# Two of four convolution tiles' input projections, and a third modulation vector, move from ahead of the attention blocks to the gaps between their heads

## The chip, the cores and the metric

The kernel runs on one core of one Trainium2 chip. Its engines are named as the profile names them: PE (TensorE, matmuls; PEld is its weight load), DVE (VectorE), ACT (ScalarE), POOL (GpSimd) and SP (SyncE, which here issues nearly all transfers). The metric is the device time of one execution in microseconds (us). Before the change three runs took 1443.88, 1449.33 and 1449.51 us, median 1449.33 us.

## What is computed

One inference step of a two-layer backbone on 640 tokens (512 latent, 128 context), width 1024, all in float32. The change touches the first (even) layer's mixer, cut here to its core:

```python
mp = _adaln(cond_ctx, w_mod[li], b_mod[li])     # six modulation vectors per layer and token group
hs = _modulate(y_s, norm_mix[li], ms[0], ms[1])
q, k, v, u = _even_split(hs, w_in)              # one input projection: 512 + 128 + 128 + 1024 columns
o_att  = _latent_attention(rope(q), rope(k), v, ck, cv, sink)   # windows of 384 or 512 keys, sink logit
o_conv = silu(_layernorm(_dwconv(a * sigmoid(gate), w, b)))     # a, gate = split(u); width 31, 512 channels
y_s = y_s + ms[2] * (concat([o_att, o_conv]) @ w_out)
y_s = y_s + ms[5] * (relu(_modulate(y_s, norm_ffn, ms[3], ms[4]) @ w1) ** 2) @ w2
```

The second (odd) layer has an RG-LRU in place of attention and convolution; both layers end with the squared-ReLU MLP. The context tokens go through the same steps, with their own modulation.

## The kernel before

Channels lie on the 128 partitions and tokens along the free dimension: `x` is 128 x 8 x 640. Float32 products are made of three matmuls on split operands (high x high, high x low, low x high), so a projection of 128 output channels, a **unit**, is 48 matmuls of 320 to 322 columns (`product`, L113, called by `att_unit`). `weights` loads the unit's 512 KB (`wraw`), ACT makes the high part (`whi`, L98), DVE the low one (`wlo`, L66).

The even layer runs in this order. The first modulation group and the norm. Then units for the four convolution tiles (two units each, value and gate), for keys, values and four query pairs: `conv_in(0)`, `conv_in(1)`, `key`, `value`, `query(0..3)`, `conv_in(2)`, `conv_in(3)`. `conv_in` multiplies the value by the sigmoid of the gate. Tiles 0 and 1 are convolved on DVE (`conv_gen`, 31 steps L409 each), tiles 2 and 3 on PE (`PE_CONV`): 16 small ACT copies (L466) bring the tile into the form `up`, and `conv_mm` runs 36 matmuls (L423; two records each in the trace) for it, 16 ACT copies (L428) take the result out.

Then five attention blocks of 128 queries: the context block first (128 keys), then latent blocks with 384, 512, 512 and 384 keys. A block goes through four head groups: `scores` (PE, six matmuls into a two-bank PSUM tile of `P2()`), `reduced` (DVE, L563: mask and running maximum, writes the scores to a slot of `S_all`), and after the fourth `softmax` (ACT: exponentials L573, scaling L579). `emit_values` of the block before it transposes the weights on PE (L599), copies them (ACT, L600, `th`) and multiplies with the values (L603); its result goes to `qh` and `ql` (ACT L606, DVE L66).

`filler(n)` takes n steps from the list `fill` between these pieces. A modulation step (`mod_gen`) is one 512 KB load `mraw` from `wmod` with two buffers, and four short matmuls (L292; eight records); 16 steps make one group of two modulation vectors. Before the change `fill` holds group (0,1), the two `conv_mm`, and group (0,2). Groups (1,0), (1,1), (1,2) of the next layer are filled into the MLP of layer 0, one step per unit. The layer norm of the convolution (`layer_norm`: ones-matmuls L627 and L645) runs in the last blocks. After attention, `out_proj` runs 16 products of 24 matmuls, 8 on the attention's result, 8 on the convolution's, and DVE adds them to `x` (L142).

`S_all` takes the two 16 KB buffers `hl` and `hh` that held the normed input, 16 slots of 512. PSUM has two tiles `p2`, one `p3` (every third `P2()` while `third()` is open) and two `p1`.

The program is written in one order, and a list scheduler settles each engine's order from it, moving instructions up where their operands are ready. On the chip each engine takes its own list in order, and waits where an operand or a buffer isn't ready.

## Time and profile before

| | us |
|---|---|
| median of three runs | 1449.33 |
| the profiled execution | 1448.39 |
| its span, first to last instruction | 1446.6 |
| mean granted TensorE clock | 0.985 of 2.4 GHz |
| the four units of `conv_in(2)` and `conv_in(3)` | 104.4 to 132.7 |
| the attention blocks | 132.7 to 256.2 |
| the output projection | 256.2 to 319.5 |
| the MLP of layer 0, its first quarter | 319.5 to 437 |

PE is busy for 1395.1 us of the span, DVE 1012.8, ACT 762.0. A stretch view gives the busy time of each engine in it, the granted clock (1.00 is 2.4 GHz, half of it 1.2 GHz), the busy share of the 16 DMA engines and what they moved. PE's busy time counts a matmul from its start to its modelled end; PEld shows how much of a stretch weights were loaded in. The chain of waits follows the last instruction back through what released each one.

### The profile page before, as it was taken

Reading aid. Unit: us, or ns where it says so; the run is one execution under the profiler, and the core shown is the slowest. Engines: PE = TensorE matmul, PEld = TensorE weight load, DVE = VectorE, ACT = ScalarE, POOL = GpSimd, SP = SyncE. Lnnn points to the kernel's source line nnn. Section 1 sums busy time; section 2 is a strip of 40 time slices with the busy share of each in tenths; the row PEclk is TensorE's granted clock in tenths of the full one; section 3 lists DMA queues with packets and bytes.
Section 4 is the critical chain, followed back from the end, with each engine's and each line's share of the span. In section 5 each row is a group of like instructions: output and inputs, shape, how many; then the busy total and the mean of one; then the engine's idle time right before and its main releaser. Section 6 shows DMA issues by size and latency. Waiting matters only on the chain.

```text
span 1446.6 us, 23553 instructions
## 1 busy us (share of the span) xinstructions
PE 1395.1 (96%) x9525; PEld 1301.3 (90%) x9525; DVE 1012.8 (70%) x1846; ACT 762.0 (53%) x1232; POOL 37.9 (3%) x57
## 2 busy tenths in 40 slices
PE   7999898999999999999999999899999999999998
PEld 4998563999989999999989999899999999999997
DVE  6699533675775675675687689997686676676673
ACT  5335788455534533543555878835643543543553
POOL 0000000000000000000000023210000000000000
PEclk9999799999999999999999999999999999999998
DMA  8623634124254334334213122122213113113112
GB/s 327 230 76 126 210 136 161 59 88 131 88 173 148 102 132 175 117 117 175 73 59 102 59 73 74 58 74 88 73 45 121 70 58 116 60 59 117 44 59 73
DMA packets 44061, 156.60 MB, mean 108 GB/s; under 512 B 5040, under 2 KB 5808, under 8 KB 43952
## 3 DMA queue, kind: packets, MB, share of 16 engines
q1 hardware_dynamic: 43952, 155.09, 30.9%
q8 instruction: 75, 1.23, 0.3%
q14 instruction: 34, 0.28, 0.1%
HBM read 152.31 MB, written 2.76 MB: 107 GB/s over the span
## 4 chain that ended last, share of the span: by engine, by line
PE 82%; DVE 7%; ACT 7%; DMA 2%; issue 1%; SPq 0%; ACTq 0%
PE p L113 65%; PE bu L113 11%; PE p L292 3%; DMA mraw<-in_wmod 2%; DVE wlo L66 1%; PE p L423 1%; DVE ib L1022 1%; DVE xc L963 1%; ACT whi L98 1%; ACT S L573 1%; PE p L603 1%; ACT z L428 1%; DVE ib L1015 1%; ACT hh L186 1%; DVE t L1014 0%
## 5 line engine op out<-in xcount | busy, mean ns | idle before, releaser
L98 ACT ACTIVATE whi<-wraw 128x512 fp32r<-128x512 f32 (+1 forms) x327 | 246.4, 779 | 440.7 <-PE p L113 323.2
L113 PE MATMUL p<-hh,whi 128*128 128x320 f32 (+1 forms) x1512 | 462.4, 313 | 2.8 <-ACT hh L186 1.7
L113 PE MATMUL p<-hl,whi 128*128 128x320 f32 (+1 forms) x1512 | 460.1, 311 | 0.2 <-DVE hl L187 0.2
L113 PE MATMUL p<-hh,wlo 128*128 128x320 f32 (+1 forms) x1512 | 350.5, 311 | 0.0
L66 DVE TENSOR_TENSOR wlo<-wraw,whi 128x512 fp32r<-128x512 f32 (+1 forms) x327 | 279.9, 879 | 48.4 <-ACT whi L98 46.9
L113 PEld LDWEIGHTS p<-hh,whi 128*128 128x128 f32 x1512 | 286.1, 189 | 15.4 <-issue 7.8
L113 PEld LDWEIGHTS p<-hl,whi 128*128 128x128 f32 x1512 | 286.4, 189 | 0.9 <-DVE hl L187 0.8
L113 PEld LDWEIGHTS p<-hh,wlo 128*128 128x128 f32 x1512 | 256.8, 189 | 0.9 <-issue 0.8
L113 PE MATMUL p<-fh,whi 128*128 128x320 f32 x528 | 166.4, 315 | 4.0 <-ACT whi L98 1.1
L113 PE MATMUL p<-fl,whi 128*128 128x320 f32 x528 | 163.3, 309 | 2.0 <-DVE fl L66 2.0
L113 PE MATMUL p<-fh,wlo 128*128 128x320 f32 x528 | 163.1, 310 | 0.7 <-DVE wlo L66 0.7
L142 DVE SCALAR_TENSOR_TENSOR x<-p,mod,x 128x320 f32<-128x320 f32 (+2 forms) x228 | 96.3, 451 | 54.6 <-PE p L113 51.7
L268 DVE TENSOR_TENSOR fr<-p,R 128x640 f32<-128x640 f32 x64 | 52.7, 823 | 101.6 <-PE p L113 101.6
L113 PE MATMUL bu<-fh,whi 128*128 128x320 f32 x360 | 112.5, 313 | 0.3 <-ACT bu L828 0.3
L113 PEld LDWEIGHTS p<-fh,whi 128*128 128x128 f32 x528 | 99.2, 188 | 14.0 <-issue 5.1
L113 PE MATMUL bu<-fl,whi 128*128 128x320 f32 x360 | 111.5, 310 | 0.0
L113 PE MATMUL bu<-fh,wlo 128*128 128x320 f32 x360 | 111.5, 310 | 0.0
L727 ACT ACTIVATE fr<-fr,bs 128x512 f32<-128x512 f32 (+1 forms) x128 | 65.2, 554 | 78.6 <-DVE bs L270 78.4
L113 PEld LDWEIGHTS p<-fl,whi 128*128 128x128 f32 x528 | 99.3, 188 | 2.4 <-DVE fl L66 2.4
L113 PEld LDWEIGHTS p<-fh,wlo 128*128 128x128 f32 x528 | 99.1, 188 | 1.5 <-DVE wlo L66 1.5
L292 PE MATMUL p<-mraw,base 128*32 128x256 f32 x768 | 66.6, 425 | 16.0 <-DMA mraw<-in_wmod 9.0
L113 PEld LDWEIGHTS bu<-fh,whi 128*128 128x128 f32 x360 | 68.0, 189 | 2.2 <-issue 1.2
(220 smaller groups left out, 1999.0 us busy)
## 6 DMA issues: line engine op xcount, KB each, us to landing
wraw<-in_w_ff SPq DMA_DIRECT2D x128, 512.0 KB, 3.5
mraw<-in_wmod SPq DMA_DIRECT2D x96, 512.0 KB, 4.2
wraw<-in_w_li SPq DMA_DIRECT2D x16, 512.0 KB, 3.4
wraw<-in_w_att SPq DMA_DIRECT2D x14, 512.0 KB, 3.6
cw<-in_w_cv SPq DMA_DIRECT2D x8, 576.0 KB, 4.3
wraw<-in_w_ao SPq DMA_DIRECT2D x8, 512.0 KB, 3.5
wraw<-in_w_lo SPq DMA_DIRECT2D x8, 512.0 KB, 3.5
x<-in_xT SPq DMA_DIRECT2D x4, 640.0 KB, 9.1
```

What stands on the lines that cost most here:

```text
L66: nc.vector.tensor_tensor(out, full, f32(hi), op=ALU.subtract)
L98: nc.scalar.activation(hi, raw, AF.Copy)
L113: nc.tensor.matmul(o, w, v, start=start, stop=stop, **kw)
L142: nc.vector.scalar_tensor_tensor(v, src[:, a:b], gate[:, n, s:s + 1], v, op0=ALU.mult, op1=ALU.add)
L186: nc.scalar.activation(h, v, AF.Copy, scale=S[:, kt, s:s + 1])
L268: nc.vector.tensor_tensor(hy(o), p[:, :, 0:320], R, op=ALU.mult)
L292: nc.tensor.matmul(p[32 * q:32 * q + 32, half * 256:half * 256 + 256], base[:, kt], raw[:, q * 256:q * 256 + 256], start=(kt == 0), stop=( ...
L423: nc.tensor.matmul(o, w[:, b], U[j][:, g, b:b + 164], start=b == 0, stop=b == 8)
L428: nc.scalar.activation(zv[32 * g:32 * g + 32, s], o[32 * s:32 * s + 32], AF.Copy)
L573: nc.scalar.activation(S[g][:, :N], S[g][:, :N], AF.Exp, bias=mx[:, g:g + 1], scale=1.0, accum_out=ss[:, g:g + 1])
L603: nc.tensor.matmul(pav[c], vv[:, sl, c], th[:, b.kv], start=(j == 0), stop=(j == len(vs) - 1))
L727: nc.scalar.activation(r[:, a:b], r[:, a:b], AF.Relu, bias=bs[:, q:q + 1])
```

## The change

- `conv_in(2)` and `conv_in(3)` leave the place ahead of attention. They become `conv_in_steps`: a step is one eighth of a unit (six matmuls), in the one tile `p3`. With the two `conv_mm` they form a second list, `work`.
- A `gap(m, w)` takes three steps of DVE's convolution, m modulation steps and w steps of `work`. It stands after every head group (before: after every second one), after every slice of `emit_values`, and after every block.
- Group (1,0) of the next layer's modulation joins `fill` ahead of attention; the MLP of layer 0 keeps (1,1) and (1,2).
- The normed input must now live through the blocks, so `S_all` is six slots of a new tile `S_own` (two of them first hold the rope table) and ten slots in `x` itself. After the last block `x` is loaded again, four 640 KB transfers on POOL's queue.
- In the blocks `p3` belongs to `work`, so scores and transposes share the two `p2`. `th` and its kin have two buffers instead of three. The convolution's weights come in 12 pieces of 192 KB a tile (four buffers), not four of 576 KB (two buffers).
- The layer norm of the convolution moves into the first half of the output projection.
- `Norm.finish` writes its two sums into one `p2` tile, where it had two `p1`, when it runs in another stage than the norm's (three times).

```diff
-    def product(p, wh, wl, cols, rhs):
+    def product(p, wh, wl, cols, rhs, first=True, last=True):
...
+            w = None if one else P2()
             for h in range(2):
-                p = P1()
-                nc.tensor.matmul(p[:, 0:320], ones, self.acc[:, h * 320:h * 320 + 320], start=True, stop=True)
-                nc.vector.tensor_scalar(v[:, h], p[:, 0:320], 1.0 / 1024, 1e-6, op0=ALU.mult, op1=ALU.add)
+                p = P1()[:, 0:320] if one else w[:, h, 0:320]
+                nc.tensor.matmul(p, ones, self.acc[:, h * 320:h * 320 + 320], start=True, stop=True)
...
+            if not one:
+                nc.vector.tensor_scalar(v, w[:, :, 0:320], 1.0 / 1024, 1e-6, op0=ALU.mult, op1=ALU.add)
...
+    S_own = bp.tile([128, 6, 512], F32, name="S")
+    rope = S_own[:, 4:6]
+    xs = x.rearrange("p k t -> p (k t)")
+    S_all = [S_own[:, i] for i in range(6)] + [xs[:, i * 512:i * 512 + 512] for i in range(10)]
...
+    def conv_in_steps(j):
+        t = []
+        for i in (2 * j, 2 * j + 1):
+            wh, wl = weights(w_att[i])
+            p = spare[0].tile([128, 2, 512], F32, name="p3", tag="p3")
+            for k in range(8):
+                product(p, wh, wl, [k], [rhs[k]], k == 0, k == 7)
+                yield
+            a = ap_.tile([128, 640], F32, name="tg", tag="t", bufs=4)
+            t += [a, normed(a, p)]
+        conv_u(j, None, None, t)
+        yield
...
-    conv_in(2)
-    conv_in(3)
-    fill.append(mod_gen(0, 1, mp))
+    use_spare.pop()
+    work.extend(conv_in_steps(j) for j in PE_CONV)
+    work.extend(conv_mm(j) for j in PE_CONV)
+    fill.extend([mod_gen(0, 1, mp), mod_gen(0, 2, mp), mod_gen(1, 0, mp)])
...
+    GAPS = [((1, 2), None, (1, 2))] + [((1, 2), (1, 1), (1, 1))] * 4
+    def gap(m, w):
+        conv_step(3)
+        filler(m)
+        filler(w, work)
+    gap(4, 4)
     for i, pair in enumerate(blocks):
         for g in range(4):
             scores(pair, g)
-            if g % 2:
-                filler(F2)
+            gap(*GAPS[i][0])
         if i:
-            emit_values(i - 1)
+            emit_values(i - 1, GAPS[i][1])
         for b in pair:
             b.softmax()
...
+        gap(*GAPS[i][2])
     conv_step(200)
-    emit_values(4)
-    filler(100)
-    for _ in ln:
-        pass
+    filler(100, work)
+    emit_values(4, (1, 0))
+    for k in range(0, 8, 2):
+        nc.gpsimd.dma_start(x[:, k:k + 2], xT[:, k:k + 2])
+    use_spare.append(1)
...
     for t in range(4):
+        next(ln, None)
         out_proj(w_ao, t, qr, lambda n, p: add_gated(n, p, G))
+        if t == 1:
+            for _ in ln:
+                pass
...
-        for g in range(3):
+        for g in range(1, 3):
             fill.append(mod_gen(1, g, mp))
```

What stands where, at three places. On PE, before, at the end of the last of the four units and the start of the context block; p3_1188 is the unit's tile, p1_1274 the modulation's, p2_1311 and p2_1326 the first two score tiles:

```order
L113 MATMUL p3_1188<-hl_157,whi_1184 128x322
L113 MATMUL p3_1188<-hh_156,wlo_1185 128x320
L113 MATMUL p3_1188<-hh_156,wlo_1185 128x322
L292 MATMUL p1_1274<-mraw_1275,base_77 32x256 x4
L292 MATMUL p1_1274<-mraw_1281,base_77 32x256 x4
L113 MATMUL p2_1311<-kh_230,qh_228 128x128 x2
L113 MATMUL p2_1311<-kl_231,qh_228 128x128 x2
L113 MATMUL p2_1311<-kh_230,ql_229 128x128 x2
L113 MATMUL p2_1326<-kh_230,qh_228 128x128 x2
```

And now, where the first score tile (p2_1043) stands inside the first of those units (p3_1018), with modulation steps (pm_987) between:

```order
L305 MATMUL pm_987<-mraw_1000,base_77 32x256 x4
L119 MATMUL p3_1018<-hh_156,whi_1014 128x322
L119 MATMUL p3_1018<-hl_157,whi_1014 128x322
L119 MATMUL p3_1018<-hh_156,wlo_1015 128x320
L119 MATMUL p3_1018<-hh_156,wlo_1015 128x322
L119 MATMUL p2_1043<-kh_230,qh_228 128x128 x2
L119 MATMUL p2_1043<-kl_231,qh_228 128x128
L305 MATMUL pm_987<-mraw_1006,base_77 32x256 x4
L119 MATMUL p2_1043<-kl_231,qh_228 128x128
L119 MATMUL p2_1043<-kh_230,ql_229 128x128 x2
L119 MATMUL p3_1018<-hh_156,whi_1014 128x320
```

The blocks begin four units earlier in PE's list, and the four units are spread to the third block; 44 modulation steps stand between them and the last transposes, where there were 32.

On ACT, before, around the first exponentials (L573): both sigmoids (L450, `sgm`) and both runs of copies `up` are done ahead of the one table load:

```order
L450 ACTIVATE sgm<-sgm,bs 128x512
L450 ACTIVATE sgm<-sgm,bs 128x128
L466 ACTIVATE up<-u 32x172 x16
L573 ACT_TABLE_LOAD
L573 ACTIVATE S,ss<-S,mx 128x128 x4
L575 ACTIVATE es<-es 128x4
L573 ACTIVATE S,ss<-S,mx 128x128 x3
L579 ACTIVATE S<-S,ss 128x128 x4
```

And now, after the context block's scaling (L618), ahead of the first latent block's exponentials (L612); `tg` is the gate:

```order
L618 ACTIVATE x<-x,ss 128x128
L104 ACTIVATE whi<-wraw 128x1024
L490 ACT_TABLE_LOAD
L490 ACTIVATE tg<-tg,bs 128x512
L490 ACTIVATE tg<-tg,bs 128x128
L506 ACTIVATE up<-u 32x172 x16
L639 ACTIVATE th<-p_1389 128x1024
L612 ACT_TABLE_LOAD
L612 ACTIVATE x,ss<-x,mx 128x384
L646 ACTIVATE qh<-p_1387 128x4x128
```

The same comes once more in the third block, so the blocks hold five table loads where they held one, and both runs of 16 copies.

On PE at the start of the MLP of layer 0, before, the norm's two sums (L209) between the first two units (p2_2864, p2_2948):

```order
L113 MATMUL p2_2864<-hh_2541,wlo_2861 128x322
L113 MATMUL bu0_2856<-hh_2541,whi_2860 128x320
L113 MATMUL bu1_2857<-hh_2541,whi_2860 128x320
L209 MATMUL p1_2918<-sq_2583,ones_70 128x320
L209 MATMUL p1_2921<-sq_2583,ones_70 128x320
L113 MATMUL p2_2948<-hh_2541,whi_2944 128x320
```

And now, the sums in a p2 tile (p2_3031); the next unit's tile (p2_3057) has the same PSUM address:

```order
L119 MATMUL bu1_2970<-hh_2654,whi_2973 128x320
L219 MATMUL p2_3031<-sq_2696,ones_70 128x320 x2
L305 MATMUL pm_2042<-mraw_3280,base_77 32x256 x4
L119 MATMUL p2_3057<-hh_2654,whi_3053 128x320
```

The second unit stands behind DVE's reading of the sums, with one modulation step between.

## Rows read from the trace of the kernel before

**Rows 1.** The head of the page: the span, busy time of PE, ACT and DVE with share and instruction count, and the clock that the throttle granted in 40 slices (tenths).

```profile
span 1446.6 us, 23553 instructions
PE 1395.1 (96%) x9525; PEld 1301.3 (90%) x9525; DVE 1012.8 (70%) x1846; ACT 762.0 (53%) x1232; POOL 37.9 (3%) x57
...
PEclk9999799999999999999999999999999999999998
```

**Rows 2.** Stretches of the four units, the blocks, the output projection and the MLP's first quarter, then the blocks in three parts: length, busy us of PE, PEld, DVE, ACT and POOL (instructions), granted clock, DMA share, GB/s.

```profile
104.40:132.70 28.30, 28.30 (x193) 28.11 (x191) 27.09 (x40) 15.11 (x26) 0.00 (x0) 1.00 0.22 75
132.70:256.20 123.50, 105.56 (x710) 62.21 (x710) 60.08 (x175) 93.97 (x209) 0.00 (x0) 0.89 0.49 170
256.20:319.50 63.30, 63.30 (x434) 63.30 (x433) 48.48 (x95) 34.34 (x50) 0.00 (x0) 1.00 0.22 75
319.50:437.00 117.50, 117.50 (x836) 108.11 (x836) 78.25 (x139) 52.73 (x85) 0.00 (x0) 1.00 0.40 134
132.70:180.00 47.30, 39.57 (x264) 24.70 (x264) 32.37 (x85) 34.40 (x87) 0.00 (x0) 0.78 0.62 216
180.00:220.00 40.00, 36.42 (x251) 23.76 (x253) 12.98 (x43) 32.55 (x68) 0.00 (x0) 0.96 0.34 123
220.00:256.20 36.20, 29.56 (x205) 13.75 (x198) 14.73 (x47) 27.03 (x57) 0.00 (x0) 0.95 0.48 160
```

**Rows 3.** Who waited for whom in the blocks (132.7 to 256): us in total, times, the longest.

```profile
ACT S L573 <- DVE mx L570: 9.1, 4, 6.2
...
ACT z L428 <- PE p L423: 7.0, 5, 3.0
...
PE p L292 <- DMA mraw<-in_wmod: 5.6, 6, 1.4
...
PE p L423 <- ACT z L428: 4.1, 5, 1.4
...
PE p L292 <- DVE mx L563: 1.9, 1, 1.9
...
PE p L113 <- DVE bs L270: 1.6, 1, 1.6
```

**Rows 4.** Pieces of the chain of waits on PE, start us and length: six units in a row; then, in the blocks, a modulation step and a group of 18 convolution records at either clock, six score matmuls, 12 records of values, eight transposes.

```profile
90.14 42.63 PE p L113 x288
...
144.30 1.01 PE p L292 x8
...
175.87 4.45 PE p L423 x18
...
180.89 2.71 PE p L423 x18
183.59 0.92 PE p L113 x6
...
216.84 2.89 PE p L603 x12
...
239.49 1.02 PE p L599 x8
...
243.37 0.57 PE p L292 x8
```

**Rows 5.** Groups on ACT in the blocks, by line and shape: busy us, mean ns of one.

```profile
L466 ACT ACTIVATE up<-u 32x172 f32<-32x172 f32 x17 | 8.7, 513 | 1.4 <-DVE u L456 1.3
...
L634 ACT ACTIVATE zsq<-z 128x656 f32<-128x656 f32 x4 | 2.8, 735 | 0.0
...
L573 ACT ACT_TABLE_LOAD x1 | 1.3, 1283 | 0.0
L98 ACT ACTIVATE whi<-wraw 128x1024 fp32r<-128x1024 f32 x1 | 1.1, 1059 | 0.0
L450 ACT ACTIVATE sgm<-sgm,bs 128x512 f32<-128x512 f32 x1 | 0.7, 722 | 1.9 <-DVE bs L270 1.9
L450 ACT ACTIVATE sgm<-sgm,bs 128x128 f32<-128x128 f32 x1 | 0.4, 387 | 0.0
```

**Rows 6.** ACT in order of time around that table load: start us, us.

```profile
145.76 1.02 ACT L466 ACTIVATE up<-u 32x172 f32<-32x172 f32 x2
146.80 1.28 ACT L573 ACT_TABLE_LOAD   x1
148.10 0.40 ACT L573 ACTIVATE S<-S,mx 128x128 f32<-128x128 f32 x1
```

**Rows 7.** Pieces of the chain in which the `mraw` load itself was waited for: start us, us from issue to landing.

```profile
133.83 5.64 DMA mraw<-in_wmod
...
220.36 3.53 DMA mraw<-in_wmod
...
232.70 4.25 DMA mraw<-in_wmod
```

**Rows 8.** The chain from the end of the blocks into the MLP of layer 0: the layer norm's sums (L627, L645), the output projection, the norm's sums (L209), units and modulation steps.

```profile
240.51 0.86 PE p L627 x2
...
241.94 0.42 PE p L627 x2
...
252.88 1.06 PE p L645 x2
...
255.80 0.42 PE p L645 x2
256.22 63.42 PE p L113 x432
...
319.93 1.08 PE p L209 x4
...
329.44 7.32 PE p L113 x48
336.76 0.57 PE p L292 x8
337.33 7.32 PE p L113 x48
```

**Rows 9.** DVE at that norm, in order of time: start us, us, idle before.

```profile
320.51 1.03 DVE L210 TENSOR_SCALAR nv<-p 128x320 f32<-128x320 f32 x2 [1.74 <-PE p L209]
```

**Rows 10.** Issues of transfers on the page: count, KB each, median us to landing.

```profile
mraw<-in_wmod SPq DMA_DIRECT2D x96, 512.0 KB, 4.2
...
x<-in_xT SPq DMA_DIRECT2D x4, 640.0 KB, 9.1
```

More of the change, by code (lines that the diff above doesn't have):

```diff
@@ L43, in backbone @@
     ps = ctx.enter_context(tc.tile_pool(name="ps", bufs=1, space=PSUM, reuse_waits="tile"))
-    spare, turn_ = [], count()
+    spare, use_spare, turn_ = [], [], count()
     @contextmanager
@@ L50, in third @@
             spare.append(pool)
+            use_spare.append(1)
             yield
             spare.pop()
+            use_spare.clear()
     def P2():
-        if spare and next(turn_) % 3 == 2:
+        if use_spare and next(turn_) % 3 == 2:
             return spare[0].tile([128, 2, 512], F32, name="p3", tag="p3")
         return ps.tile([128, 2, 512], F32, name="p2", tag="p2", bufs=2)
+    ones_, both_ = count(), []
     def P1():
-        return ps.tile([128, 512], F32, name="p1", tag="p1", bufs=2)
+        t = "p1b" if both_ and next(ones_) % 2 else "p1"
+        return ps.tile([128, 512], F32, name="p1", tag=t)
     def f32(ap):
@@ L113, in mm @@
         nc.tensor.matmul(o, w, v, start=start, stop=stop, **kw)
-    def product(p, wh, wl, cols, rhs):
+    def product(p, wh, wl, cols, rhs, first=True, last=True):
         n = len(cols)
         for i, (c, ((ha, hb), (la, lb))) in enumerate(zip(cols, rhs)):
-            s, e = i == 0, i == n - 1
+            s, e = first and i == 0, last and i == n - 1
             cs = slice(c * 128, c * 128 + 128)
@@ L281, in backbone @@
     nc.vector.tensor_tensor(base[:, :, 0:2], sg, cv, op=ALU.mult)
-    MOD, SC = {}, {}
+    MOD, SC, done_ = {}, {}, set()
     def mod_tile(l, g):
         MOD[l, g] = const.tile([128, 16, 2], F32, name=f"mod{l}{g}")
-        return P1()
+        return ps.tile([128, 512], F32, name="pm", tag="p1b")
     def mod_mm(p, raw, half, kt):
@@ L316, in mod_gen, with filler @@
                     mod_finish(l, g, half, p, pool)
+                    done_.add((l, g, 1 - half))
                 yield
-    fill = []
-    def filler(n):
+    fill, work = [], []
+    def filler(n, fill=fill):
         while n and fill:
@@ L338, in first_mods @@
         for kt in ks:
-            raw = (bp if kt % 2 else mp).tile([128, 1024], F32, name="mraw", tag="m" if kt % 2 else "mraw", bufs=3 if kt % 2 else NM)
+            raw = (bp if kt % 2 else mp).tile([128, 1024], F32, name="mraw", tag="m" if kt % 2 else "mraw", bufs=2)
             nc.sync.dma_start(raw, wmod[0, 0, half, kt])
@@ L443, in conv_in, with conv_u @@
     def conv_in(j):
-        pa, pg = [first[i] if i < 3 else att_unit(i) for i in (2 * j, 2 * j + 1)]
-        ta = ap_.tile([128, 640], F32, name="ta", tag="t", bufs=4)
-        ba = normed(ta, pa)
-        sgm = ap_.tile([128, 640], F32, name="sgm", tag="t", bufs=4)
-        bg = normed(sgm, pg)
+        return conv_u(j, *[first[i] if i < 3 else att_unit(i) for i in (2 * j, 2 * j + 1)])
+    def conv_in_steps(j):
[10 more added lines that the diff above has]
+        yield
+    def conv_u(j, pa, pg, done=None):
+        if done:
+            ta, ba, sgm, bg = done
+        else:
+            ta = ap_.tile([128, 640], F32, name="ta", tag="t", bufs=4)
+            ba = normed(ta, pa)
+            sgm = ap_.tile([128, 640], F32, name="sgm", tag="t", bufs=4)
+            bg = normed(sgm, pg)
         for q, (a, b) in enumerate(SEG):
@@ L588, in scores, with emit_values @@
             b.reduced(g, p[:, b.kv, 0:b.N])
-    def emit_values(n):
+    def emit_values(n, fills):
         pair = blocks[n]
@@ L594, in emit_values @@
         for j, sl in enumerate(vs):
[L595 removed]
+            th = bp.tile([128, 2, 512], F32, name="th", tag="m", bufs=2)
             pt = P2()
@@ L603, in emit_values @@
                 nc.tensor.matmul(pav[c], vv[:, sl, c], th[:, b.kv], start=(j == 0), stop=(j == len(vs) - 1))
+            gap(*fills)
         pv4 = pav.rearrange("p (g t) -> p g t", g=4)
@@ L673, in backbone @@
     ln = layer_norm()
-    fill.extend(conv_mm(j) for j in PE_CONV)
-    fill.append(mod_gen(0, 2, mp))
-    filler(F1)
+    def gap(m, w):
[3 more added lines that the diff above has]
+    gap(4, 4)
     for i, pair in enumerate(blocks):
```

31 lines of the change are left out of this document (16 added, 15 removed).

## The prediction

> **What bounds the kernel now.** I read the head of the page first: PE is busy for 96% of the span, at full clock except early [rows 1]. So time comes from work taken off PE where it is the bound, or from a stretch where PE is not well used. The stretches show which is which [rows 2]. In the four units, the output projection and the MLP, PE is busy without a break at clock 1.00, and in the first two the weight loads fill the stretch as well: there a removed matmul is removed time. The blocks, 123.5 us, are another thing: PE counts 105.56 us busy, but weights are loaded in only 62.21, the clock is 0.89, ACT is busy for 93.97 (76%), and nobody is full. The waits say why [rows 3]: ACT waits for DVE's maxima (9.1 us) and for PE's convolution (7.0), PE for `mraw` loads (5.6) and for ACT's copies (4.1). Each engine takes its list in order and stands at the other's result. The change moves the four units and 12 more modulation steps into this stretch.
>
> **PE's work in the blocks.** Prices are taken at full clock from the chain [rows 4]. Now: 32 steps at 0.57, eight convolution groups at 2.71, 15 sets of eight transposes at 1.02, 60 records of values at 2.89 for 12, 20 score groups at 0.92 or less: 18.2 + 21.7 + 15.3 + 14.5 + 18.4 = 88 us of 123.5. The change adds four units, 42.63 / 6 = 7.1 each, 28.4, and 12 steps, 6.8: 123 us. They start at 104.4, so PE alone could be done at 104.4 + 123.4 = 228, against 256.2.
>
> **ACT's work.** It has 94.0 us in the blocks [rows 2]. To this come [rows 5] the copies of the first tile that now lie before 132.7 (15 x 0.513 = 7.7), its sigmoid (0.72 + 0.39 = 1.1), four more table loads (4 x 1.283 = 5.1), two more weight splits (2.1); the layer norm's squares leave (2.8): 107.2 us. The first exponentials can start when the context block's four score groups are done: one unit 7.1, seven steps 4.0, four groups at most 3.7, then DVE: about 120. So ACT alone could be done at 227. The two floors coincide; the end depends on how well queues in order interlock. ACT's share was 0.76 over the blocks, 0.73, 0.81 and 0.75 in their three parts [rows 2]. Of its 29.5 idle us the longest single wait, 6.2 us for a maximum [rows 3], lies in the first part, where the clock was 0.78 and a modulation step took 1.01 us instead of 0.57, a convolution group 4.45 instead of 2.71 [rows 4]. Now units stand between the scores there and feed PE. Walking ACT's new list by hand with these durations, waiting for PE and DVE where it must, I come to about 244 (share 0.87); hand-over times are left out of it. I take 0.85: 120 + 107.2 / 0.85 = 246. **The blocks end 10.1 us earlier.** Bounds: 0.76, as now, gives 261 (4.9 later); 0.92 gives 236.5 (19.7 earlier).
>
> A table load lasts 1.28 us in the trace, and the first exponential follows at 148.10, 0.02 after its end; the copies before it end at 146.78, 0.02 ahead [rows 6]. By the Trainium skill ("ScalarE: Activation LUTs", What ACT_TABLE_LOAD costs) every switch to another set costs a drain of some 1.38 us besides, 2.66 in all. By it the four loads would be 10.6 us, ACT 112.7, the blocks' end 252.6 and the total 1444; the trace shows no such drain, and I give that 0.03, inside the second rival's chance.
>
> **Modulation.** Of the 16 steps of group (1,0), 12 go into the blocks; four stay behind them. In the MLP a unit takes 7.32 and the step after it 0.57 with nothing hidden [rows 8]: **12 x 0.57 = 6.8 us gained.** In the blocks two buffers set the pace: an `mraw` load took 3.5 to 5.6 us from issue to landing where it was waited for [rows 7], 4.2 in the median [rows 10], so a pair of steps needs about 5 to 6 us and 44 steps 110 to 132 us of the 142 that I forecast. That is close but not the bound; it is part of why I don't take 0.92. If the pace were 6.5 a pair, the end would be at 247 by this alone. The queue of SP is in order, but the loads for weights and convolution that stand between wait for buffers released long before.
>
> **The norm's sums.** Three times `Norm.finish` now fills a p2 tile. At both MLPs the next unit's tile lies on the same address, so PE stands until DVE has read the sums. Today PE goes straight on after them [rows 8], and DVE's two reads take 1.03 us [rows 9]. One read of 640 columns with the hand-over is about 1.3 us; the first MLP has a 0.57 step to put in: **0.7 + 1.3 = 2.0 us lost.** In the RG-LRU a third tile is open and nothing waits.
>
> **The layer norm and the reload of x.** The ones-matmuls, 0.86 + 0.42 + 1.06 + 0.42 = 2.8 us [rows 8], move to the output projection, which is full; the first pair falls into the wait for the last values, so **2.2 us lost.** Behind them DVE and ACT have 28 us (eight products of 24 matmuls at 63.42 / 432 = 0.147 each) for a chain of about 25 by the same walk; in the order the first convolution product is interleaved with its neighbour as operands come, so I count at most 1 us there. The reload can start when the last transposes have read x, and DVE's additions to x, with DVE's list behind them, wait for it. PE has two products (7 us) and the last values (2) before it needs a tile back. The nearest price is the first load of x, 9.1 us [rows 10], on SP's queue; POOL's has no row. Bounds: 0, and 9 at twice that landing. **I take 2.0 for both**, by the nearest row. The skill's page on POOL-issued transfers ("DMA: Bandwidth & Descriptors", Anatomy of one DMA) gives 2.0 us plus bytes over 436 GB/s; estimated from it the four would land in 8 us and cost nothing; no row here shows it.
>
> On DVE 32 convolution steps now stand behind the first scores, where 18 stood; busy for 60 of 123.5 us [rows 2] it stays below both others. Fewer buffers for `th` and scores are in the share above.
>
> **Sum.** -10.1 - 6.8 + 2.0 + 2.2 + 2.0 = -10.7. From the profiled execution's 1448.4 (span 1446.6; 0.9 under the median of the runs): **1438 us.**
>
> **Rivals.**
> - *The blocks fill better.* If the interleaved units keep PE at full clock and ACT always has something ready, share 0.92: 19.7 + 0.6 = 20.3 us, 1428. For it: the largest wait sat in the slow stretch. Against: no part of the blocks was above 0.81, and the sigmoids stand in ACT's list ahead of copies and exponentials that could run. Chance 0.20.
> - *The gain is eaten.* The share stays near 0.76 to 0.81, because scores and transposes now turn on two tiles instead of three and each waits for DVE or ACT to empty one: 1452 at 0.76, 1444 at 0.81. For it: the waits are mutual, and nothing shortens a chain from scores to values. Chance 0.26.
> - *PE becomes the bound at a low clock: slower.* In the blocks PE's busy share times its clock was 0.855 x 0.89 = 0.76. In the first part, with single waits of PE up to 1.9 us [rows 3], the clock was 0.78 [rows 2], and the new order can leave such waits at each `mraw` and `th`. Units at half clock cost 14 us instead of 7. If PE is used no better than 0.76 with 123.4 us to do, the blocks end at 266.8, 10.6 later: 1458. It decides from 0.77 downwards. For it: the clock of 0.78 in the first part; against: a unit is 48 matmuls with no wait inside a step. Chance 0.14.
>
> **How the numbers follow.** My case (share 0.82 to 0.89) has 0.40. A measurement of this kernel tells about 0.5% (7.2 us) from no change. Faster by more: the first rival, and my case above 0.83: 0.55. Within: the second rival and the rest of my case, 0.31. Slower: the third rival, 0.14. The range goes from the first rival's time to the second's upper end, 1427 to 1453; it leaves out the third rival and a tail beyond 0.92.
>
> **What would show it.** Right: the blocks end at 240 to 252 with ACT busy some 107 us from the first exponential on and above 0.8; units and scores alternate on PE at a clock of at least 0.95 up to about 165; the MLP of layer 0 holds 33 steps or so, its units without a step lasting 7.3; about 1 us of PE waiting for DVE after the norm's sums at each MLP; five table loads of 1.28 us. Wrong: PE waiting for `mraw` for more than 10 us in the blocks; a clock under 0.85 there; PE or DVE standing for more than 3 us at the reload of x; ACT below 0.8 with its waits on `mx` or the convolution grown.

## The result and the profile after

The changed kernel takes **1466.5 us** in the median of four runs (1463.9 to 1468.9), the kernel before 1448.9 on the same chip: a ratio of **1.0129, interval 1.0099 to 1.0159**. It is slower by 17.6 us where 10.7 were to be gained. Its profiled execution took 1468.9 (span 1467.1), 2.4 above its median.

The table sets the ends of the stretches in the two profiled executions side by side. The first row is the first modulation step behind the query units (after) and the start of the four units (before), the others are the end of the last values matmul, DVE's first read of the norm's sums at each block, and the last instruction.

| | before | after | difference |
|---|---|---|---|
| attention's work begins | 104.4 | 108.3 | +3.9 |
| last values matmul | 255.8 | 275.3 | +19.5 |
| norm's sums, MLP of layer 0 | 320.5 | 344.1 | +23.6 |
| norm's sums, RG-LRU | 792.1 | 814.2 | +22.1 |
| norm's sums, MLP of layer 1 | 1002.9 | 1023.6 | +20.7 |
| last instruction | 1443.3 | 1463.6 | +20.3 |

The 3.9 us at the start are this execution's own: six other versions below run the same program up to that point, and their profiled executions begin there at 103.9 to 105.5. So the blocks with the units inside take 167.0 us where units and blocks took 151.4 before, and that is the loss. The output projection adds 4.1, the first MLP gives back 1.5.

The page's head, with the clock in 40 slices, answers to [rows 1].

```profile
span 1467.1 us, 23597 instructions
...
PE 1402.4 (96%) x9525; PEld 1301.9 (89%) x9525; DVE 1011.8 (69%) x1843; ACT 766.6 (52%) x1236; POOL 36.4 (2%) x61
...
PEclk9999989999999999999998999999999999999998
```

The head hardly differs: a stretch that got longer by a tenth doesn't show in a share of the whole. The stretch view, columns as in [rows 2], does: the blocks, the output projection, the MLP's first quarter, the blocks in three parts, and last the blocks from the first table load for an exponential on.

```profile
108.40:275.30 166.90, 141.00 (x996) 86.91 (x996) 80.57 (x204) 111.20 (x233) 2.24 (x4) 0.93 0.56 189
275.30:342.90 67.60, 67.60 (x461) 64.84 (x462) 54.83 (x107) 37.27 (x54) 0.00 (x0) 1.00 0.31 108
342.90:460.40 117.50, 117.15 (x826) 109.41 (x826) 79.00 (x140) 52.54 (x85) 0.00 (x0) 1.00 0.37 123
108.40:160.00 51.60, 44.55 (x341) 30.82 (x342) 42.43 (x95) 29.46 (x68) 0.00 (x0) 0.93 0.55 185
160.00:220.00 60.00, 49.63 (x346) 31.88 (x347) 27.91 (x74) 47.45 (x97) 0.00 (x0) 0.91 0.55 180
220.00:275.30 55.30, 46.83 (x314) 24.21 (x313) 10.22 (x36) 34.30 (x70) 2.24 (x4) 0.94 0.59 202
...
123.50:275.30 151.80, 127.34 (x881) 77.06 (x874) 67.02 (x178) 106.94 (x227) 2.24 (x4) 0.92 0.55 184
```

ACT has 106.9 us of work from there on, almost to the us what the prediction counted (107.2), but needs 151.8 us for it: a share of 0.70, not 0.85. PE is idle for 25.9 of 166.9 us; before it was idle for 17.9 of the 151.8 us of units and blocks [rows 2]. The units were to fill PE's gaps, and the gaps grew. Who is waited for, as in [rows 3], with SP's queue, which issues the loads, behind PE's and ACT's rows:

```profile
ACT z L449 <- PE p L444: 13.4, 6, 3.7
...
PE pm L305 <- DMA mraw<-in_wmod: 13.0, 9, 3.6
...
ACT th L639 <- PE p L638: 10.5, 4, 5.5
ACT whi L104 <- PE p L119: 10.0, 4, 4.7
...
PE p L642 <- ACT th L639: 4.7, 3, 3.7
```

```profile
SPq L326 <- PE pm L305: 91.8, 41, 8.5
SPq L326 <- DMA mraw<-in_wmod: 23.8, 18, 4.0
SPq L443 <- PE p L444: 23.2, 19, 5.2
```

PE waits 13.0 us for `mraw` where it waited 5.6 [rows 3], and ACT's large waits are now for PE. SP's first row says how: 41 times it stood at a modulation load until PE had used the buffer, so the load starts only when the step two places earlier in PE's list is done. Before, from 104.4 to 256 us, it stood so 26 times (L313 and L292 are these lines there):

```profile
SPq L313 <- PE p L292: 55.4, 26, 10.8
```

In the changed kernel's chain, start us and length:

```profile
109.80 5.05 DMA mraw<-in_wmod
...
115.60 4.44 DMA mraw<-in_wmod
...
158.94 4.07 DMA mraw<-in_wmod
...
226.50 4.25 DMA mraw<-in_wmod
...
257.79 7.16 DMA mraw<-in_wmod
```

The last of these is the longest, and PE's longest wait for a load, 3.6 us, ends with it. It started while the first three transfers of the reload of x were under way (POOL's row: start us, us, engine); from 257 to 265 us the DMA engines were busy throughout:

```profile
255.21 1.73 POOL L734 DMA_DIRECT2D x<-in_xT  x3 [253.61 <-PE p L638]
```

```profile
257.00:265.00 8.00, 3.33 (x31) 1.73 (x29) 0.94 (x3) 3.03 (x8) 0.00 (x0) 0.97 1.00 400
```

The second place is the end of layer 0's MLP. The chain there in the changed kernel, then the same place in a version that differs only in a counter (a_turn, below):

```profile
797.06 0.82 DVE sq L205
797.88 0.47 DVE x L148
798.36 0.14 issue
798.49 3.55 PE bu L119 x12
```

```profile
791.26 3.85 PE p L119 x26
795.11 1.76 PE bu L119 x12
796.86 1.61 PE p L119 x11
```

PE waits 3.63 us for DVE's addition to x; then twelve matmuls take 3.55 us, against 1.76 without that wait. The granted clock is 0.50 from there to 807.0, the lower of its two levels:

```profile
798.50:807.00 8.50, 7.64 (x27) 7.27 (x28) 3.56 (x6) 2.59 (x4) 0.28 (x6) 0.50 0.16 60
```

Summed from start to start over 798.9 to 807.0, the matmuls take 3.0 us more than at 0.147 each. In a_turn 26 matmuls of the RG-LRU's first product stand where PE waits in the changed kernel.

### The profile page after: what moved, and what is told of

It is laid out like the page before. It is cut to its first block, busy times and chain, and to the rows that moved or that the text cites. A ratio compares the mean times of both kernels' runs of the same rounds, so it can differ in the third digit from the quotient of the medians.

```text
span 1467.1 us, 23597 instructions
## 1 busy us (share of the span) xinstructions
PE 1402.4 (96%) x9525; PEld 1301.9 (89%) x9525; DVE 1011.8 (69%) x1843; ACT 766.6 (52%) x1236; POOL 36.4 (2%) x61
## 4 chain that ended last, share of the span: by engine, by line
PE 81%; DVE 7%; ACT 7%; DMA 3%; issue 1%; POOL 0%; SPq 0%; ACTq 0%; POOLq 0%
PE p L119 64%; PE bu L119 11%; DMA mraw<-in_wmod 3%; PE pm L305 3%; DVE wlo L72 1%; PE p L444 1%; ACT up L506 1%; DVE ib L1069 1%; ACT z L449 1%; ACT whi L104 1%; PE p L642 1%; DVE xc L1010 1%; DVE t L1061 0%; DVE ib L1062 0%; PE p L272 0%
## 5 line engine op out<-in xcount | busy, mean ns | idle before, releaser
L305 PE MATMUL pm<-mraw,base 128*32 128x256 f32 x768 | 69.7, 421 | 22.8 <-DMA mraw<-in_wmod 22.7
```

The lines of the kernel that those rows point to most:

```text
L305: nc.tensor.matmul(p[32 * q:32 * q + 32, half * 256:half * 256 + 256], base[:, kt], raw[:, q * 256:q * 256 + 256], start=(kt == 0), stop=( ...
```

## The experiments

All runs are compared with the kernel before on the same chip, whose median lay between 1448.3 and 1449.8, so two versions from different chips can differ by some 1.5 us for that alone; a time is the median, in brackets the interval of its ratio. "Last values" is the end of the last values matmul in the profiled execution, which can lie some us off the median, "MLP" the time from the norm's sums of the MLP of layer 0 to those of the RG-LRU.

| version | us | ratio (interval) | last values | MLP |
|---|---|---|---|---|
| before | 1448.9 | 1 | 255.8 | 471.6 |
| after | 1466.5 | 1.0129 (1.0099 to 1.0159) | 275.3 | 470.1 |
| a_early | 1464.5 | 1.0114 (1.0096 to 1.0131) | 271.3 | 470.1 |
| a_mods32 | 1466.9 | 1.0130 (1.0109 to 1.0151) | 269.7 | 470.6 |
| a_ahead | 1464.7 | 1.0121 (1.0101 to 1.0141) | 278.2 | 461.5 |
| a_up | 1459.6 | 1.0081 (1.0064 to 1.0098) | 264.9 | 469.1 |
| a_noload | 1447.1 | 0.9992 (0.9979 to 1.0006) | 258.9 | 462.0 |
| a_ahead32 | 1466.8 | 1.0119 (1.0102 to 1.0136) | 273.7 | 464.2 |
| a_best | 1464.3 | 1.0102 (1.0086 to 1.0118) | 267.5 | 470.6 |
| b_m2 | 1449.6 | 1.0002 (0.9990 to 1.0014) | 256.7 | 472.9 |
| a_turn | 1462.0 | 1.0093 (1.0072 to 1.0113) | 271.8 | 462.2 |
| b_turn | 1452.3 | 1.0020 (1.0004 to 1.0036) | 256.7 | 475.9 |
| a_deep | 1456.1 | 1.0040 (1.0022 to 1.0058) | 265.8 | 463.9 |
| a_fix | 1450.7 | 1.0005 (0.9987 to 1.0022) | 262.5 | 460.8 |
| a_ahead_deep | 1448.8 | 1.0002 (0.9985 to 1.0019) | 264.9 | 456.7 |
| a_ahead_best | 1446.2 | 0.9977 (0.9966 to 0.9989) | 258.6 | 457.9 |
| a_noload_fix | 1441.8 | 0.9951 (0.9932 to 0.9970) | 259.1 | 457.5 |
| a_fix_late | 1448.6 | 1.0000 (0.9986 to 1.0015) | 264.1 | 456.8 |
| a_best3 | 1452.9 | 1.0026 (1.0015 to 1.0037) | 263.2 | 461.0 |
| a_best_e | 1439.3 | 0.9938 (0.9921 to 0.9956) | 253.9 | 457.5 |

Two theories stood at the start. **A**: two 512 KB buffers for the modulation loads hold PE. **B**: ACT's runs of 16 layout copies (8.4 us each) hold what PE and DVE need.

**a_early.** Early modulation loads in six buffers, the score tile split into three tiles for it.

```diff
-            raw = (bp if kt % 2 else mp).tile([128, 1024], F32, name="mraw", tag="m" if kt % 2 else "mraw", bufs=2)
+            pool, t, n = ((mp, "mraw", 2), (bp, "m", 2), (bp, f"s{kt // 3 % 2}", 1))[kt % 3]
+            raw = pool.tile([128, 1024], F32, name="mraw", tag=t, bufs=n)
...
-    S_own = bp.tile([128, 6, 512], F32, name="S")
-    rope = S_own[:, 4:6]
+    S_a = bp.tile([128, 2, 512], F32, name="S", tag="s0")
+    S_b = bp.tile([128, 2, 512], F32, name="S", tag="s1")
+    rope = bp.tile([128, 2, 512], F32, name="rope")
```

> The changed kernel, with the first layer's early modulation loads in six buffers instead of four: the two spare score tiles, still empty then, take loads too. Theory that the early slip comes from the third "m" buffer that the change takes away (TensorE waits 9.6 us for mraw before 108 us, 3.4 before): the slip of about 4 us goes, 1462 to 1463 us. If the early slip has another cause: 1466 us.

Measured 1464.5; the two intervals overlap almost wholly, so by itself it shows nothing.

**a_mods32.** The next layer's group back beside the MLP.

```diff
-    fill.extend([mod_gen(0, 1, mp), mod_gen(0, 2, mp), mod_gen(1, 0, mp)])
+    fill.extend([mod_gen(0, 1, mp), mod_gen(0, 2, mp)])
...
-        for g in range(1, 3):
+        for g in range(3):
```

> The changed kernel, with the next layer's first modulation group (1,0) back beside the MLP: 32 steps in the blocks in place of 48. Theory A, modulation loads that TensorE waits for fill the blocks' gaps with waits (13.0 us on mraw, the longest of 7.2 near 258): the waits of the last blocks go, some 8 us, and the MLP gets back at most 2 us: 1458 to 1461 us. Theory B, ScalarE's runs of copies in the middle hold the blocks: 1465 to 1469 us, no gain.

Measured 1466.9, no gain. The trace says why this is a weak test: the scheduler still put 38 steps ahead of the last values (44 in the changed kernel), since the MLP's first loads go out early. Six steps fewer, 2.7 us less from first step to last values, and 39.5 steps instead of 32.5 in the MLP.

**a_ahead.** The projections back ahead of attention.

```diff
+    conv_in(2)
+    conv_in(3)
     use_spare.pop()
-    work.extend(conv_in_steps(j) for j in PE_CONV)
```

> The changed kernel, with the input projections of conv tiles 2 and 3 back ahead of attention; the rest of the change stays (48 modulation steps, scores partly in x and its reload, a conv accumulator of its own, norm sums in one two-bank tile). Theory A, the modulation steps carry the loss: most of it stays, about 1460 us. Theory B, the projections with their splits, sigmoids and copies between the heads carry it: 1450 us or a little below.

Measured 1464.7: the loss stays with the projections out of the blocks. Its chain from 137 to 278 us, by line, is the clearest view of theory A; PE's waits for the loads, 16.6 us in 17, stand first among PE's.

```profile
by line: DMA mraw<-in_wmod 35.0%; PE pm L305 13.7%; PE p L444 12.1%; ACT z L449 9.1%; PE p L643 7.2%; ACT up L506 5.8%; PE p L639 5.0%; PE p L119 3.8%; issue 1.7%; ACT S L613 0.8%; DVE x L603 0.8%; DVE wlo L72 0.8%; ACT x L613 0.8%; PE p L6
```

```profile
PE pm L305 <- DMA mraw<-in_wmod: 16.6, 17, 4.2
PE p L444 <- ACT z L449: 9.5, 7, 5.4
```

**a_up.** The copies four at a time.

```diff
-            for g in range(4):
-                for s in range(4):
-                    nc.scalar.activation(up[32 * s:32 * s + 32, g], uv[32 * g:32 * g + 32, s], AF.Copy)
+            def ups(g):
+                for s in range(4):
+                    nc.scalar.activation(up[32 * s:32 * s + 32, g], uv[32 * g:32 * g + 32, s], AF.Copy)
+            pend.extend([lambda g=g: ups(g) for g in range(4)])
...
                 next(fill[0])
                 n -= 1
+                if fill is work and pend:
+                    pend.pop(0)()
```

> The changed kernel, with the 16 copies that lay out each conv tile for TensorE issued four at a time behind the next four steps of the conv work, in place of 16 in a row (8.4 us of ScalarE each time). Theory B, the runs of copies hold the split and transposed tiles back and TensorE's clock falls behind them: 6 to 8 us come back, about 1459 us. Theory A, the modulation loads: 1465 to 1468 us.

Measured 1459.6, 6.9 off, as theory B had it. So neither theory alone holds.

**a_noload.** One tile loaded once for all three groups.

```diff
-                raw = pool.tile([128, 1024], F32, name="mraw", tag="mraw", bufs=NM)
-                nc.sync.dma_start(raw, wmod[l, g, half, kt])
+                if (l, g) in ((1, 1), (1, 2)) or not once:
+                    raw = pool.tile([128, 1024], F32, name="mraw", tag="mraw", bufs=NM)
+                    nc.sync.dma_start(raw, wmod[l, g, half, kt])
+                    once.append(raw)
+                else:
+                    raw = once[0]
```

> The changed kernel without 47 of the 48 modulation loads beside the blocks: the three groups (0,1), (0,2) and (1,0) are all computed from one tile that is loaded once, so these modulations are not the reference's; TensorE's work is the same. It prices the waits on these loads. Theory A (loads bind): the 13.0 us that TensorE waits for mraw in the blocks come back, and what queues behind, 1452 us or less. Theory B (ScalarE's copies): at most 4 us come back, 1462 us or more, since the same stalls are then filled by the wait for ScalarE.

Measured 1447.1: 19.4 us are gone with the loads, more than the whole loss. The stretch from the first step to the last values is 152.6 us, with the same instructions on ACT as after:

```profile
106.30:258.90 152.60, 134.07 (x1044) 87.80 (x1043) 80.85 (x206) 111.24 (x233) 2.24 (x4) 0.97 0.21 64
```

It is the strongest evidence for theory A. The blocks are 14.4 us shorter: PE's idle time in them falls from 25.9 to 18.5, and its busy time from 141.0 to 134.1 with six steps more, at a clock of 0.97 instead of 0.93. The gain isn't all in the blocks: those six steps, which the scheduler, free of loads, also placed ahead of the last values, have left the MLP, which is 8 us shorter. But the time is only that of the kernel before; the gain that was forecast doesn't come with the loads gone. PE's largest waits in the blocks are then for copies and for DVE's reading of a finished group:

```profile
PE p L448 <- ACT z L453: 6.1, 6, 1.7
PE p L646 <- ACT th L643: 5.4, 5, 3.0
PE pm L305 <- DVE mt L310: 4.6, 2, 4.4
```


**a_ahead32** joins a_ahead and a_mods32.

> The projections of conv tiles 2 and 3 ahead of attention, as in the kernel before, and 32 modulation steps in the blocks in place of 48. With the projections ahead, the chain of the 48-step version is 33.8% mraw loads (of 146 us, about 49 us). If the loads bind wherever the projections do not cover them, it gains 8 to 12 us against that version: 1453 to 1457 us. If the blocks are held by something else (two score accumulators, ScalarE): 1462 to 1466 us, as 32 steps gave nothing in the changed kernel.

Measured 1466.8, a miss for theory A as I had put it. 42 steps still lie ahead of the last values here, so the number of loads was hardly cut; what matters is how they are buffered (a_deep).

**a_best** joins a_early, a_up and a_mods32.

> The changed kernel with three edits at once: six early buffers, the copies four at a time, and 32 modulation steps. If the gains add (2, 7 and 0 us): 1457 to 1458 us. If the 16 saved steps count once ScalarE is out of the way: 1450 us or less.

Measured 1464.3, not below a_up alone but 4.7 above it, at the edge of what the intervals tell apart: the gains don't add. The MLP has 39.5 steps instead of 32.5 again, and the blocks are no shorter than a_up's (163.4 against 161.0).

**b_m2.** In the kernel before, the tag "m" at its three places (early loads, rotation, `th`).

```diff
-        t1 = bp.tile([128, 512], F32, name="rt1", tag="m", bufs=3)
+        t1 = bp.tile([128, 512], F32, name="rt1", tag="m", bufs=2)
```

> The kernel before with two "m" buffers in place of three, one part of the change alone (early modulation loads, the rotation's scratch, transposed weights). If the early slip comes from it: 1452 us (3 to 4 us slower). If not: 1449 us.

Measured 1449.6, no difference: without the third buffer the kernel before loses nothing. The slip of 3.9 us belongs to the profiled execution, as the starts of the six other versions say.

**a_turn, b_turn.** One line ahead of the RG-LRU, in the changed kernel and in the kernel before.

```diff
+    next(turn_)
     lru = ExitStack()
```

> The changed kernel with the counter that picks every third accumulator advanced by one ahead of the LRU block, nothing else. In the changed kernel the LRU's first product falls on the third tile, whose banks are those that the MLP's last sums still occupy: TensorE waits 3.63 us at 794.9 and runs 3.0 us longer at half clock behind it; the kernel before and the versions with the projections ahead (counter 70 and 33 there, 29 here) have no such wait. If that is the cause: 6 to 7 us come back, 1460 us. If the wait comes from the changed norm sums or from VectorE's order: 1465 to 1467 us.

> The kernel before with the same counter advanced by one ahead of the LRU block (70 to 71), so that there too the first product falls on the third tile. If the turn of that counter is the cause: 6 to 7 us slower, 1455 us. If not: 1449 us.

Measured 1462.0 and 1452.3: 4.5 gained, and 2.5 lost in the kernel before (1449.8 on the same chip). The MLP shrinks from 470.1 to 462.2 us and the wait of 3.6 is gone. Behind it a part is given back: a_turn has a wait of 1.8 at 818 with 1.6 us of lower clock behind it, where the changed kernel has one of 1.2 at 829. In the kernel before the turned counter doesn't make the same wait; it puts one of 6.0 at 805.7 (PE for DVE's L964) where 1.8 was. So the counter's place matters in both, not always by the same wait.

**a_deep.** Eight more load buffers, in the room of `hh` and `hl`, from the end of the last projection step on.

```diff
+                if deep:
+                    raw = deep[next(ring) % 8]
+                else:
+                    raw = pool.tile([128, 1024], F32, name="mraw", tag="mraw", bufs=NM)
...
         conv_u(j, None, None, t)
+        if j == 3:
+            for n in ("hh", "hl"):
+                q = hp.tile([128, 4, 1024], F32, name="mraw", tag=n)
+                deep.extend(q[:, i] for i in range(4))
```

> The changed kernel with eight buffers more for the modulation loads from the point at which the conv projections are done (near 180 us), in the room of the split activations that nobody reads from there on; all loads are made. Theory A, two buffers with a load's latency between them hold TensorE: most of what the version without loads gained in the second half of the blocks comes back, 1455 to 1459 us. Rival, the loads compete for the DMA engines: at 0.60 busy share before, nothing, 1465 us.

Measured 1456.1, 10.5 off, with every load made. (Its profiled execution, 1452.8, is the fastest of its seven.) The third part of the blocks shows it best: it lasts 45.8 us instead of 55.3, with PE at full clock, against 0.94, and the wait of 3.6 us beside the reload of x is gone.

```profile
105.60:160.00 54.40, 45.97 (x364) 31.70 (x365) 46.45 (x105) 33.51 (x77) 0.00 (x0) 0.97 0.59 194
160.00:220.00 60.00, 50.41 (x340) 32.53 (x342) 24.58 (x63) 46.19 (x92) 0.00 (x0) 0.91 0.68 237
220.00:265.80 45.80, 42.75 (x319) 23.23 (x319) 9.85 (x37) 31.42 (x66) 2.24 (x4) 1.00 0.51 167
```

The transfers ran at 237 GB/s in the middle part, 180 in the changed kernel: contention for the DMA engines falls as the cause of the whole. At the one place where they were full, beside the reload of x, a load did take 7.16 us.

**a_fix** joins a_up, a_deep and a_turn (and gives the buffers back ahead of the next norm, as a_deep does).

> Three of these edits at once on the changed kernel: copies four at a time, eight buffers more from 180 us on, the counter advanced by one. If their gains (7, 8 and 6 us) are of different waits they add: 1445 us, a little below the kernel before. If the copies and the loads are the same stalls: 1452 us.

Measured 1450.7: 15.8 off, where the three alone sum to 21.9. The overlap is put down to copies and loads, for which a_noload_fix speaks. The loss is made good, but the kernel is no faster than before.

**a_ahead_deep.** a_ahead with the eight buffers from the start of the blocks.

```diff
     use_spare.pop()
+    for n in ("hh", "hl"):
+        q = hp.tile([128, 4, 1024], F32, name="mraw", tag=n)
+        deep.extend(q[:, i] for i in range(4))
```

> Projections of conv tiles 2 and 3 ahead of attention, as in the kernel before, all else as changed, and eight buffers more for the modulation loads through all of the blocks. The version with the projections ahead and two buffers takes 1464.7 us. If its loss is the wait for loads (33.8% of the chain through its blocks): 1449 to 1453 us, and so the projections between the heads bring nothing that these buffers do not bring without them. If it is the score accumulators or the order between the heads: 1458 us or more.

**a_ahead_best.** The same with a_up's edit, but the first group's copies at once.

```diff
+            ups(0)
+            pend.extend([lambda g=g: ups(g) for g in range(1, 4)])
```

> The same with the layout copies four at a time behind the conv steps that need them. TensorE waits 5.4 us for the run of copies at 145 us in the version with the projections ahead: 3 to 5 us faster than without this edit, about 1446 us. If that wait is covered by something else: no change.

Measured 1448.8 and 1446.2; on the same chip all twelve runs of the second lie below the median of the first, so the 2.6 us are a gain. a_ahead loses 15.9 us to its two buffers. With both edits the projections ahead of attention are 4.5 us better than between the heads (a_fix). They have the extra buffers some 40 us earlier, and ran on another chip (3.8 when each is set against the kernel before on its own), so I don't count all of the 4.5; but no gain of the interleaving shows. The blocks and then PE's waits in them:

```profile
136.00:258.60 122.60, 111.35 (x843) 60.15 (x843) 63.13 (x187) 97.58 (x213) 2.25 (x4) 0.94 0.73 253
```

```profile
PE p L449 <- ACT z L454: 7.0, 7, 1.7
PE p L449 <- DVE bs L283: 3.2, 1, 3.2
PE pm L305 <- DMA mraw<-in_wmod: 1.9, 1, 1.9
```

50 steps are done in these 122.6 us, 32 in the 123.5 before [rows 2]: here the gaps do take steps in; the MLP has 29 of them instead of 48 and is 13.7 us shorter than before.

**a_noload_fix** joins a_noload, a_up and a_turn.

> The changed kernel with 47 of 48 modulation loads left out (all three groups computed from one tile, so these modulations are not the reference's), the copies four at a time and the counter advanced by one. The floor of this order: without the loads alone 1447.1 us. If copies and turn still pay when no load is waited for: 1447 less 4.5 less up to 7, 1436 to 1443 us. If the copies only mattered because they delayed the steps behind the loads: 1442 to 1443 us.

Measured 1441.8: 5.3 below a_noload, 4.5 of it in the MLP, where the counter acts; the blocks are not shorter (155.2 against 152.6 from the first step to the last values). With no loads to wait for, splitting the runs of copies gains nothing in the blocks: what a_up gained, it gained together with the loads.

**a_fix_late.** a_fix with the steps of the first two blocks put into the later ones.

```diff
-    GAPS = [((1, 2), None, (1, 2))] + [((1, 2), (1, 1), (1, 1))] * 4
+    GAPS = [((0, 2), None, (0, 2)), ((0, 2), (1, 1), (1, 1))] + [((2, 2), (2, 1), (1, 1))] * 3
...
-    gap(4, 4)
+    gap(2, 4)
```

> The version with copies four at a time, eight more buffers from 180 us and the counter advanced by one (1450.7 us), with the modulation steps of the first two blocks, which still wait in two buffers, put into the later blocks, two at a head. If the waits of the first half (about 5 us on mraw before 160 us) go and the later gaps take the steps in: 1445 us. If the later blocks have no room for them: 1450 us or more.

Measured 1448.6; against a_fix it is unclear. The blocks end 1.6 later, 160.2 us after their first step instead of 157.1, and the MLP is 4.0 shorter.

**a_best3.** a_ahead_best with the third accumulator in the scores' rotation.

```diff
-        pz = spare[0].tile([128, 2, 512], F32, name="p3", tag="p3")
+        pz = P2()
...
     conv_in(3)
-    use_spare.pop()
```

> The fastest version so far (projections ahead, eight more load buffers, copies four at a time: 1446.2 us) with the third accumulator back in the rotation of the scores and transposes, from which the conv matmuls take their tile too, as in the kernel before. If the accumulator that the change takes from the scores costs anything here: 2 to 5 us faster. If not: 1445 to 1447 us.

Measured 1452.9, 6.7 slower: with the projections ahead, the conv accumulator of its own, a part of the change, is a gain. With one rotation for all, PE's scores wait for DVE's maxima, a row that a_ahead_best's list doesn't have:

```profile
PE p L119 <- DVE mx L612: 5.9, 4, 3.8
```

**a_best_e.** a_ahead_best with a_early's edit.

> The fastest version so far (1446.2 us) with six early load buffers in place of four. The same edit on the changed kernel took 2.1 us off, inside the interval. If the early loads bind: 1444 us. If the difference was noise: 1446 to 1447 us.

Measured **1439.3**, 0.9938 of the kernel before (0.9921 to 0.9956): the fastest, below both kernels. It gains 6.8 on a_ahead_best (6.1 when each is set against the kernel before on its own chip). In the profiled execution, 2.9 us under its median, the first scores start only 0.7 us earlier (131.9 against 132.6), but the stretch from there to the last values is 4.0 us shorter and the output projection 2.4. So the earlier start is only a small part of it. The edit also splits the score tile into three; which of the two does it was not separated.

## Why the prediction was wrong

**The step that failed** is "I take 0.85: 120 + 107.2 / 0.85 = 246". The work was right: ACT had 106.9 us, five table loads of 1.28, and the first of them for an exponential started at 123.5 (118.8 in a_up, without the slip). The share was 0.70, and the blocks ended at 275.3, some 271 without this execution's slip. The walk by hand let ACT wait for PE and DVE, but gave PE its modulation steps as if loaded.

The loads are the larger part of this miss, not the whole. From first step to last values 142 us were forecast and 167 measured; without the loads it is 152.6, so some 14 of the 25 us go with them and 11 stay; the six steps more that were done there are 3.4 of PE's work. a_noload, from its first table load for an exponential on:

```profile
118.90:258.91 140.01, 121.48 (x928) 78.06 (x921) 68.25 (x181) 106.88 (x227) 2.24 (x4) 0.96 0.22 66
```

ACT's share is 0.76 there: the 0.85 was too high with no load to wait for, and the blocks are no shorter than the 151.4 us of units and blocks before. What is left is the share of now, 0.76, at which the second rival put it ("the waits are mutual"). Which of the waits holds it there no run separates; the cause of this part stays open.

**Where that came from**: "a pair of steps needs about 5 to 6 us and 44 steps 110 to 132 us of the 142 ... That is close but not the bound". It compared a mean pace with a mean demand. The steps don't come evenly: the order puts four in a row, 188.1 to 195.8 us, with waits of 1.6, 2.2 and 0.5 among them, and others three and four us apart. A load of 4 to 5 us, as in the chain above, that starts when its buffer is released is late for each of those, and PE, in order, holds units, scores and transposes behind it. Without the loads 19.4 us come back, with eight more buffers in the second half 10.5. The prediction's own sign for this, PE waiting for `mraw` for more than 10 us, came out at 13.0; that row understates it, since ACT's and DVE's waits for PE behind each stop are booked elsewhere. Its other sign, ACT below 0.8 with its waits for the convolution grown, came out too: 13.4 us against 7.0 [rows 3]. The sentence that loads for the convolution on SP's queue wait for buffers released long before was wrong: SP stood at them for 23.2 us, and the modulation loads stood behind.

**Modulation in the MLP**, 6.8 to be gained: the mechanism was right. The MLP had 32.5 steps instead of 48, 15.5 x 0.57 = 8.8 us. But it became only 1.5 shorter. The rest went into a wait that the prediction didn't look for: the change takes the blocks' tiles out of the count that gives every third accumulator to the third tile, the RG-LRU's first product falls on that tile (the count is 29 there, 2 modulo 3, where it was 70, 1 modulo 3), and PE waits 3.6 us and runs 3.0 longer at the lower clock. a_turn shows it: the MLP falls to 462.2, though of the 6.6 us only 4.5 come back in the whole time.

**The norm's sums**, 2.0 lost: right in kind, mis-sized. PE waited 0.3 at the first MLP and 0.9 at the second, none at the RG-LRU.

**The layer norm's sums**, 2.2 lost: the output projection grew by 4.1 us. 3.25 modulation steps in it are 1.9, which leaves 2.2 for the sums. **The chain and the reload**, 2.0: nothing in the output projection. PE is busy for 67.60 of 67.60 us; the four POOL transfers landed after 6.3 us in the median, while PE still had products to do. But the first three of them went out before the last block's end, and the modulation load beside them took 7.16 us, with PE waiting 3.6 for it. The versions with two buffers and the projections between the heads all show this (7.1 to 7.6 us, waits of 3.4 to 3.9), a_deep and a_fix don't. So the reload most likely did cost some 3 us, inside the blocks, a price that the prediction didn't look for there; no run moves the reload alone.

**The rivals.** "PE becomes the bound at a low clock" named the right side and about half the size (1458, some 9 us slower, against 17.6): the 123.4 us of PE's work at full clock took 167, a use of 0.74, under its 0.76. Its mechanism was half right: the waits at the loads came, 13.0 of PE's 25.9 idle us, but the clock was 0.93, above the 0.89 of before. "The gain is eaten" named the share at which a_noload ends, and had two tiles for the scores as its reason; a_best3 speaks against that reason, but with the projections ahead. No run gave the scores a third tile with the projections between the heads. The drain that the Trainium skill ("ScalarE: Activation LUTs", What ACT_TABLE_LOAD costs) adds to a table load doesn't show here either: the next exponential starts 0.01 us after the load's end.

```profile
189.35 0.60 ACT L646 ACTIVATE qh<-p 128x512 fp32r<-128x512 f32 x1
189.97 1.28 ACT L612 ACT_TABLE_LOAD   x1
191.26 0.72 ACT L612 ACTIVATE x<-x,mx 128x512 f32<-128x512 f32 x1
```

Open: what holds ACT at 0.76 without the loads; what of a_best_e's gain is the early loads and what the split of the score tile; and how much of the 4.5 us between a_fix and a_ahead_best is the place of the projections.

## What to carry to other kernels

Filling an in-order engine's gaps with steps that each need a fresh load only works if the load is there: check the shortest distance between steps against a load's latency and the buffers ahead of it, not the mean. Look for room that falls free in the same stretch; here eight buffers in the dead split activations took back the whole loss (1464.7 to 1448.8) without the interleaving. And when a share is forecast for an engine, ask what it would be if one wait were gone: here it was 0.70 with the loads and 0.76 without, never 0.85. When a change adds or removes tiles from a rotation, see which tile the next block's first product falls on; a counter shifted by one was worth 2.5 to 4.5 us, far from the edit.

## What the hardware showed that I had not expected

A wait of 3.6 us on PE was followed by a stretch at the lower clock (granted clock 0.50; twelve matmuls 3.55 us, not 1.76), which cost 3.0 us more, so that the wait cost nearly twice its length. The DMA engines were far from full at the changed kernel's 0.56 busy share and 189 GB/s: a_ahead_best, with more buffers, ran its blocks at 0.73 and 253 GB/s. They were full for 8 us beside the reload of x, at 400 GB/s. Between executions of one program up to the same instruction the start of the blocks lay 4.5 us apart (103.9 to 108.3), so single profiles can't be compared to the us.
